# Rotary embedding and attention scores: the first batch loaded into a stage buffer, loads issued behind stores, q transposed early and k late in a step

## The chip, the cores and the metric

One core of a Trainium2 chip runs the whole program. The metric is the device time in microseconds (us) of one execution, the lower the better; a kernel's time is the median of several executions. Engines are named as the profile names them: PE (TensorE; PEld is its weight load), DVE (VectorE), ACT (ScalarE), POOL (GpSimd), SP (SyncE, which here does nothing but issue DMAs).

## What is computed

q and k have 16 batches, 512 positions, 16 heads and 64 numbers per head, all float32. Both get the rotary embedding, with one table of cosines and one of sines (512 positions by 32), and then every query position of a batch is multiplied with every key position, head by head:

```python
q1, q2 = q[..., :32], q[..., 32:]
q_rot = np.concatenate([q1 * cos - q2 * sin, q1 * sin + q2 * cos], axis=-1)
# k_rot: the same of k
scores = np.einsum('bshd,bthd->bsht', q_rot, k_rot)   # (16, 512, 16, 512), float32
```

The inputs are 67 MB in all and the output is 268 MB: four bytes leave the core for each that enters it.

## The kernel before

**Tiles and steps.** A *block* of q or k is 128 positions of one batch with all 16 heads, 128 partitions by 1024 numbers. There are 4 blocks in a batch (`C` = 4), and 64 in all (`NST`). Step `i` computes the scores of q block `i` against all 512 keys of its batch, in 8 pieces (`p` = 0 to 7, two heads each): `scores(i, p, st)` does two matmuls into one of three PSUM tiles `ps`, ACT copies that to the stage tile `st` (L166), and after the last piece SP issues one 4 MB store of `st` to the output (L171). There are three stage tiles, `stage_pool`, of 4 MB each; they are used in turn, and the first copy of a step waits until the store that last read its tile has landed.

**The first batch** is cut the other way. Its q and k are cut into four *units* of 4 heads each with all positions, so that the first scores need only one unit of each; a step's output is then stored in four parts of 1 MB (L169). The units are loaded by eight DMAs of 512 KB, `load_unit` (L79), into the same input tiles that later hold pairs of blocks.

**Loads.** From the second batch on, `load_pair` (L88) loads two neighbouring blocks with one DMA of 1 MB: into one of three tiles for k (`k_in`), one of two for q (`q_in`). A load waits until the embedding of the two blocks that were in the tile before is done.

**The embedding** of a block, `rope` (L115, L118, L121), is three DVE instructions: times cosine, times signed sine into `part`, and the sum. The signed sines, `ss_k` and `ss_q`, are made at the start by `build_table`, two small DVE instructions each (L59, L60).

**Transposes.** `transposed` turns 4 pieces of 128x128 of an embedded block on PE into a PSUM tile `bank` (there are two of them), which is then copied to `qT_t` or `kT_t`; a block takes two of these. In the first four steps `tr_act` does both halves of a unit, and ACT copies them (L176). From step 4 on DVE copies them (L259, in the first batch L215 for the key blocks of the second batch).

**The order of the work is written out by hand** (`tc.manual_schedule()`), and each engine runs its instructions in the order in which the program names them. SP issues DMAs in that order too, so a DMA that has to wait holds up those behind it. In steps 4 to 63 the order is: the load of this step (q at odd `i`, k at even `i`), then the eight pieces, with a transposed half after the pieces 0, 2, 3 and 5 (k, k, q, q), each followed by one embedding instruction on DVE and DVE's copy, and the rest of the embedding (q block `i`+2 and k block `i`+5) at the end. Within each step SP therefore has the load ahead of the store.

Of the kernel before, what the change touches and what calls it, by code (L numbers as in the profile page):

```python
# [10 lines left out]
def kernel(  # L11
# [8 lines left out]
    nc = tc.nc  # L20
# [5 lines left out]
    HD = D // 2  # L26
# [29 lines left out]
    def build_table(which):  # L56

        ss = const_pool.tile([P, C, 2, HD], fp32, name=f"ss_{which}")
        nc.vector.tensor_copy(out=ss[:, :, 0, :], in_=tabs["sin", which])  # L59
        nc.vector.tensor_scalar_mul(ss[:, :, 1, :], tabs["sin", which], -1.0)  # L60
        tabs["ss", which] = ss.rearrange("p c x j -> p c (x j)")

    in_tiles = {}
# [2 lines left out]
    def in_tile(which, pair):  # L66
        t = in_pool.tile(
            [P, 2, H * D], fp32, tag=which + "_in", bufs=IN_BUFS[which], name=which + "_sb"
        )
        in_tiles[which, pair] = t  # L70
        return t

    def load_unit(which, u):

        t = in_tiles.get((which, u // 2))
        if t is None:
            t = in_tile(which, u // 2)
        src = (k_v if which == "k" else q_v)[0, :, :, G * u : G * (u + 1), :]
        nc.sync.dma_start(t[:, u % 2].rearrange("p (c h d) -> p c h d", c=C, h=G), src)  # L79

    def load_pair(which, pair):

        b, x = divmod(pair, C // 2)
        if b >= B:
            return
        t = in_tile(which, pair)
        src = (k_v if which == "k" else q_v)[b, :, 2 * x : 2 * x + 2]
        nc.sync.dma_start(t.rearrange("p c (h d) -> p c h d", h=H), src)  # L88
# [3 lines left out]
    def rope(which, n):  # L92


        src = in_tiles[which, n // 2][:, n % 2]
        a = rot_pool.tile([P, H * D], fp32, tag="rot_" + which, name=which + "_rot")
        bt = rot_pool.tile([P, H * D], fp32, tag="part", name="part")
        cs, ss = tabs["cos", which], tabs["ss", which]
        if n < C:
            v1 = "p (c g j) -> p c g j"  # L100
            k1 = {"c": C, "j": HD}
            cs = cs.unsqueeze(2).to_broadcast((P, C, 2 * G, HD))
            ss = ss.unsqueeze(2).to_broadcast((P, C, G, D))
            k2 = {"c": C, "j": D}
        else:
            v1 = "p (g j) -> p g j"
            k1 = {"j": HD}
            cs = cs[:, n % C].unsqueeze(1).to_broadcast((P, 2 * H, HD))
            ss = ss[:, n % C].unsqueeze(1).to_broadcast((P, H, D))
            k2 = {"j": D}  # L110
        swapped = bass.AP(bt.tensor, bt.offset + HD, [bt.ap[0], (D, H), (-HD, 2), (1, HD)])
        a4 = a.rearrange("p (h x j) -> p h x j", x=2, j=HD)
        rots[which, n] = a
        return [
            lambda: nc.vector.tensor_tensor(  # L115
                a.rearrange(v1, **k1), src.rearrange(v1, **k1), cs, op=mult
            ),
            lambda: nc.vector.tensor_tensor(  # L118
                bt.rearrange(v1, **k2), src.rearrange(v1, **k2), ss, op=mult
            ),  # L120
            lambda: nc.vector.tensor_tensor(a4, a4, swapped, op=add),  # L121
        ]
# [50 lines left out]
    def tr_act(which, n):  # L173
        for g in range(2):
            bank, dst = transposed(which, n, g)
            nc.scalar.copy(out=dst, in_=bank)  # L176

    def run(ops):
        for op in ops:
            op()  # L180

    with tc.manual_schedule():
        load_tables("k", "(c p) j -> p c j")
        load_tables("q", "(p c) j -> p c j")
        for u in range(2):
            load_unit("k", u)
            load_unit("q", u)
        for which in ("k", "q"):
            for u in range(2, C):
                load_unit(which, u)  # L190
        load_pair("k", 2)
        make_identity(nc, ident)
        build_table("k")
        run(rope("k", 0))
        tr_act("k", 0)
        build_table("q")
        run(rope("q", 0))
        tr_act("q", 0)


        for i in range(C):
            st = stage_pool.tile([P, H, S], fp32, tag="stage", name="st")
            late = []
            if i > 0:
                late = [("k", C + i - 1, 0), ("k", C + i - 1, 1)]
            if i < C - 1:
                dve = rope("k", i + 1) + rope("q", i + 1) + rope("k", C + i)
            else:
                dve = rope("q", C) + rope("k", C + i) + rope("q", C + 1) + rope("k", 2 * C)
            for p in range(HP):  # L210
                scores(i, p, st)
                if p in (1, 2) and late:
                    bank, dst = transposed(*late.pop(0))
                    dve.pop(0)()
                    nc.vector.tensor_copy(out=dst, in_=bank)  # L215
                if p == 5:
                    run(dve[: 3 if i == 0 else 1])
                    dve = dve[3 if i == 0 else 1 :]
                    tr_act(*(("k", i + 1) if i < C - 1 else ("q", C)))
                if p == 7:  # L220
                    run(dve[:3])
                    dve = dve[3:]
                    tr_act(*(("q", i + 1) if i < C - 1 else ("k", C + i)))
            run(dve)
            if i == 0:
                load_pair("k", 3)
                load_pair("q", 2)
            elif i == 2:
                load_pair("k", 4)
                load_pair("q", 3)  # L230
                load_pair("k", 5)
            elif i == 3:
                load_pair("q", 4)
                load_pair("k", 6)


        for i in range(C, NST):
            tr = []
            if i + C < NST:
                tr += [("k", i + C, g) for g in range(2)]  # L240
            if i + 1 < NST:
                tr += [("q", i + 1, g) for g in range(2)]
            dve = []
            if i + 2 < NST:
                dve += rope("q", i + 2)
            if i + 1 + C < NST:
                dve += rope("k", i + 1 + C)
            if i % 2 == 1:
                load_pair("q", (i + 1) // 2 + 2)
            else:  # L250
                load_pair("k", (i + 4) // 2 + 3)
            st = stage_pool.tile([P, H, S], fp32, tag="stage", name="st")
            for p in range(HP):
                scores(i, p, st)
                if p in (0, 2, 3, 5) and tr:
                    bank, dst = transposed(*tr.pop(0))
                    run(dve[:1])
                    dve = dve[1:]
                    nc.vector.tensor_copy(out=dst, in_=bank)  # L259
            run(dve)  # L260


# [28 lines left out]
```

## Time and profile before

| what | before |
|---|---|
| median of 5 runs | 811.45 us (810.88 to 812.91) |
| the profiled execution, its own time | 811.71 us |
| span in its profile, first to last instruction | 809.9 us |
| PE busy | 677.5 us (84%) |
| DVE busy | 598.5 us (74%) |
| ACT busy | 500.7 us (62%) |
| bytes moved by DMA | 336.31 MB, 415 GB/s over the span |
| mean granted clock of PE | 0.951 |

How to read it: an engine's busy time is the union of its instructions' times. A table of windows gives, for stretches of the span, each engine's busy time and number of instructions, then the granted PE clock, the mean busy share of the 16 DMA engines, and the GB/s that they moved; in short windows the share can exceed 1, since a packet is counted where it starts. The chain of waits follows the execution back from its last instruction to what released each step.

### The profile page before, as it was taken

Reading aid. Unit: us, or ns where it says so; the run is one execution under the profiler, and the core shown is the slowest. Engines: PE = TensorE matmul, PEld = TensorE weight load, DVE = VectorE, ACT = ScalarE, POOL = GpSimd, SP = SyncE. Lnnn points to the kernel's source line nnn. Section 1 sums busy time; section 2 is a strip of 40 time slices with the busy share of each in tenths; the row PEclk is TensorE's granted clock in tenths of the full one; section 3 lists DMA queues with packets and bytes.
Section 4 is the critical chain, followed back from the end, with each engine's and each line's share of the span. In section 5 each row is a group of like instructions: output and inputs, shape, how many; then the busy total and the mean of one; then the engine's idle time right before and its main releaser. Section 6 shows DMA issues by size and latency. Waiting matters only on the chain.

```text
span 809.9 us, 7781 instructions
## 1 busy us (share of the span) xinstructions
PE 677.5 (84%) x3072; PEld 296.3 (37%) x3072; DVE 598.5 (74%) x624; ACT 500.7 (62%) x533; POOL 0.7 (0%) x6
## 2 busy tenths in 40 slices
PE   4997999888888888797988978888888879799870
PEld 2443444333333333343333433333333333344320
DVE  7798888887787787877868868678778787787300
ACT  3884777657556566575566656665656657566770
POOL 0000000000000000000000000000000000000000
PEclk9998999999999999999999999999999999999995
DMA  8999999999999999999999999999999999999994
GB/s 278 390 423 394 420 430 422 430 426 434 426 432 434 426 431 434 424 434 429 428 430 432 429 430 432 425 431 433 427 433 428 415 424 437 428 354 437 428 416 196
DMA packets 29028, 336.31 MB, mean 415 GB/s; under 512 B 3392, under 2 KB 7744, under 8 KB 15424
## 3 DMA queue, kind: packets, MB, share of 16 engines
q1 hardware_dynamic: 27648, 335.55, 98.2%
q8 instruction: 24, 0.39, 0.2%
q10 hardware_dynamic: 1344, 0.26, 0.2%
q14 instruction: 12, 0.10, 0.0%
HBM read 67.37 MB, written 268.44 MB: 415 GB/s over the span
## 4 chain that ended last, share of the span: by engine, by line
DMA 59%; PE 21%; DVE 8%; ACT 8%; issue 1%; ACTq 0%
DMA out_dram<-st 58%; PE ps L159 15%; ACT st L166 8%; PE bank L136 6%; DVE part L118 3%; DVE k_rot L121 2%; DVE k_rot L115 1%; DVE q_rot L121 1%; DVE q_rot L115 1%; DVE qT_t L259 1%; DMA sin_k<-in_sin_dram 0%; DVE kT_t L215 0%; ACT kT_t L176 0%; ACTq L286 0%; ACTq L166 0%
## 5 line engine op out<-in xcount | busy, mean ns | idle before, releaser
L166 ACT COPY st<-ps 128x1024 f32<-128x1024 f32 x512 | 489.5, 1021 | 275.6 <-DMA out_dram<-st 174.0
L159 PE MATMUL ps<-kT_t,qT_t 64*128 64x512 f32 x2048 | 528.8, 638 | 72.3 <-ACT st L166 69.8
L159 PEld LDWEIGHTS ps<-kT_t,qT_t 64*128 64x128 f32 x2048 | 182.3, 193 | 255.8 <-issue 148.5
L259 DVE COPY qT_t<-bank 128x512 f32<-128x512 f32 x118 | 81.5, 691 | 136.3 <-PE bank L136 135.8
L136 PE MATMUL bank<-ident,k_rot 128*128 128x128 f32 x512 | 84.5, 290 | 35.5 <-DVE k_rot L121 35.5
L136 PEld LDWEIGHTS bank<-ident,k_rot 128*128 128x128 f32 x512 | 55.0, 143 | 132.6 <-DVE k_rot L121 69.0
L136 PEld LDWEIGHTS bank<-ident,q_rot 128*128 128x128 f32 x512 | 58.9, 150 | 101.6 <-issue 78.9
L259 DVE COPY kT_t<-bank 128x512 f32<-128x512 f32 x112 | 77.0, 688 | 24.1 <-PE bank L136 24.1
L136 PE MATMUL bank<-ident,q_rot 128*128 128x128 f32 x512 | 90.6, 305 | 1.9 <-DVE q_rot L121 1.9
L121 DVE TENSOR_TENSOR k_rot<-k_rot,part 128x1024 f32<-128x1024 f32 x64 | 78.4, 1225 | 2.1
L121 DVE TENSOR_TENSOR q_rot<-q_rot,part 128x1024 f32<-128x1024 f32 x64 | 77.8, 1216 | 0.2
L115 DVE TENSOR_TENSOR q_rot<-q_sb,cos_q 128x1024 f32<-128x1024 f32 x64 | 77.9, 1218 | 0.0
L118 DVE TENSOR_TENSOR part<-k_sb,ss_k 128x1024 f32<-128x1024 f32 x64 | 77.8, 1216 | 0.0
L115 DVE TENSOR_TENSOR k_rot<-k_sb,cos_k 128x1024 f32<-128x1024 f32 x64 | 77.8, 1216 | 0.0
L118 DVE TENSOR_TENSOR part<-q_sb,ss_q 128x1024 f32<-128x1024 f32 x64 | 77.7, 1214 | 0.0
L176 ACT COPY kT_t<-bank 128x512 f32<-128x512 f32 x10 | 5.6, 619 | 6.5 <-PE bank L136 6.5
L176 ACT COPY qT_t<-bank 128x512 f32<-128x512 f32 x10 | 5.6, 617 | 2.6 <-PE bank L136 2.6
L215 DVE COPY kT_t<-bank 128x512 f32<-128x512 f32 x6 | 4.1, 684 | 4.1 <-PE bank L136 4.1
L59 DVE COPY ss_k<-sin_k 128x128 f32<-128x128 f32 x1 | 0.2, 227 | 5.2 <-DMA sin_k<-in_sin_dram 5.2
L176 ACT ACT_TABLE_LOAD x1 | 1.3, 1283 | 2.9 <-issue 2.9
masks.py:199 POOL TENSOR_SCALAR_AFFINE_SELECT ident<-ident 128x128 f32<-128x128 f32 x1 | 0.3, 293 | 0.1
L60 DVE TENSOR_SCALAR ss_k<-sin_k 128x128 f32<-128x128 f32 x1 | 0.2, 220 | 0.0
(7 smaller groups left out, 1.0 us busy)
## 6 DMA issues: line engine op xcount, KB each, us to landing
out_dram<-st SPq DMA_DIRECT2D x60, 4096.0 KB, 27.8
k_sb<-in_k_dram SPq DMA_DIRECT2D x30, 1024.0 KB, 19.9
q_sb<-in_q_dram SPq DMA_DIRECT2D x30, 1024.0 KB, 28.1
out_dram<-st SPq DMA_DIRECT2D x16, 1024.0 KB, 9.7
k_sb<-in_k_dram SPq DMA_DIRECT2D x4, 512.0 KB, 7.4
q_sb<-in_q_dram SPq DMA_DIRECT2D x4, 512.0 KB, 8.7
cos_k<-in_cos_dram ACTq DMA_DIRECT2D x1, 64.0 KB, 4.1
sin_k<-in_sin_dram ACTq DMA_DIRECT2D x1, 64.0 KB, 3.9
```

What stands on the lines that cost most here:

```text
L59: nc.vector.tensor_copy(out=ss[:, :, 0, :], in_=tabs["sin", which])
L60: nc.vector.tensor_scalar_mul(ss[:, :, 1, :], tabs["sin", which], -1.0)
L115: lambda: nc.vector.tensor_tensor(a.rearrange(v1, **k1), src.rearrange(v1, **k1), cs, op=mult),
L118: lambda: nc.vector.tensor_tensor(bt.rearrange(v1, **k2), src.rearrange(v1, **k2), ss, op=mult),
L121: lambda: nc.vector.tensor_tensor(a4, a4, swapped, op=add),
L136: nc.tensor.transpose(bank[:, x, :], src, ident)
L159: nc.tensor.matmul(out=ps[:, r, :], lhsT=lhs[64 * r : 64 * r + 64, :], rhs=rhs[64 * r : 64 * r + 64, :], start=True, stop=True,)
L166: nc.scalar.copy(out=st[:, 2 * p : 2 * p + 2, :], in_=ps)
L176: nc.scalar.copy(out=dst, in_=bank)
L215: nc.vector.tensor_copy(out=dst, in_=bank)
L259: nc.vector.tensor_copy(out=dst, in_=bank)
```

## The change

There are five parts to it.

1. `load_units` replaces `load_unit`: the first batch is loaded by four DMAs (4 heads of k, 4 of q, then the other 12 heads of k, 12 of q) into `early`, which takes the third stage tile. The input tiles are therefore free at the start, and the loads of k pair 2, q pair 2 and k pair 3 stand right behind the units on SP; k pair 4 and q pair 3 follow among the stores of step 0, k pair 5 behind step 1.
2. The two signed sine tables are built by ACT, both ahead of the first embedding.
3. In steps 0 to 3 the transposes of the next units come after the pieces 2 and 6 instead of 5 and 7, those of the second batch's keys after 0 and 1 instead of 1 and 2.
4. In steps 4 to 63 q is transposed after the pieces 1 and 3 and k after 5 and 6, and k's halves are copied by ACT instead of DVE.
5. In steps 4 to 63 the load is issued at the end of the step, behind its store on SP.

```diff
     def build_table(which):
         ss = const_pool.tile([P, C, 2, HD], fp32, name=f"ss_{which}")
-        nc.vector.tensor_copy(out=ss[:, :, 0, :], in_=tabs["sin", which])
-        nc.vector.tensor_scalar_mul(ss[:, :, 1, :], tabs["sin", which], -1.0)
+        nc.scalar.copy(out=ss[:, :, 0, :], in_=tabs["sin", which])
+        nc.scalar.mul(ss[:, :, 1, :], tabs["sin", which], -1.0)
...
+    st_first = [stage_pool.tile([P, H, S], fp32, tag="stage", name="st") for _ in range(2)]
+    early = stage_pool.tile([P, 2 * C * H * D], fp32, tag="stage", name="early")
+    units = {}
+
+    def load_units(which, head, heads):
+        n = C * heads * D
+        t = early[:, load_units.used : load_units.used + n]
+        load_units.used += n
+        t = t.rearrange("p (c e) -> p c e", c=C)
+        src = (k_v if which == "k" else q_v)[0, :, :, head : head + heads, :]
+        nc.sync.dma_start(t.rearrange("p c (h d) -> p c h d", d=D), src)
+        for h in range(0, heads, G):
+            units[which, (head + h) // G] = t[:, :, D * h : D * (h + G)]
...
-        for u in range(2):
-            load_unit("k", u)
-            load_unit("q", u)
-        for which in ("k", "q"):
-            for u in range(2, C):
-                load_unit(which, u)
+        for head, heads in ((0, G), (G, H - G)):
+            load_units("k", head, heads)
+            load_units("q", head, heads)
         load_pair("k", 2)
+        load_pair("q", 2)
+        load_pair("k", 3)
         make_identity(nc, ident)
         build_table("k")
+        build_table("q")
         run(rope("k", 0))
         tr_act("k", 0)
-        build_table("q")
...
         for i in range(C):
...
-                if p in (1, 2) and late:
+                if p in (0, 1) and late:
                     bank, dst = transposed(*late.pop(0))
                     dve.pop(0)()
                     nc.vector.tensor_copy(out=dst, in_=bank)
-                if p == 5:
-                    run(dve[: 3 if i == 0 else 1])
-                    dve = dve[3 if i == 0 else 1 :]
-                    tr_act(*(("k", i + 1) if i < C - 1 else ("q", C)))
-                if p == 7:
-                    run(dve[:3])
-                    dve = dve[3:]
-                    tr_act(*(("q", i + 1) if i < C - 1 else ("k", C + i)))
+                if i == 0 and p == 1:
+                    load_pair("k", 4)
+                if i == 0 and p == 3:
+                    load_pair("q", 3)
+                if p in (2, 6):
+                    m = len(dve) - (6 if p == 2 else 3) + (-3 if i == C - 1 else 0)
+                    run(dve[:m])
+                    dve = dve[m:]
+                    tr_act(*nxt.pop(0))
             run(dve)
-            if i == 0:
-                load_pair("k", 3)
-                load_pair("q", 2)
-            elif i == 2:
-                load_pair("k", 4)
-                load_pair("q", 3)
+            if i == 1:
                 load_pair("k", 5)
...
         for i in range(C, NST):
-            tr = []
+            tr = {}
+            if i + 1 < NST:
+                tr[1], tr[3] = ("q", i + 1, 0), ("q", i + 1, 1)
             if i + C < NST:
-                tr += [("k", i + C, g) for g in range(2)]
-            if i + 1 < NST:
-                tr += [("q", i + 1, g) for g in range(2)]
+                tr[5], tr[6] = ("k", i + C, 0), ("k", i + C, 1)
...
-            if i % 2 == 1:
-                load_pair("q", (i + 1) // 2 + 2)
-            else:
-                load_pair("k", (i + 4) // 2 + 3)
             st = stage_pool.tile([P, H, S], fp32, tag="stage", name="st")
             for p in range(HP):
                 scores(i, p, st)
-                if p in (0, 2, 3, 5) and tr:
-                    bank, dst = transposed(*tr.pop(0))
+                if p not in tr:
+                    continue
+                bank, dst = transposed(*tr[p])
+                if tr[p][0] == "q":
                     run(dve[:1])
                     dve = dve[1:]
                     nc.vector.tensor_copy(out=dst, in_=bank)
+                else:
+                    nc.scalar.copy(out=dst, in_=bank)
             run(dve)
+            if i % 2 == 1:
+                load_pair("q", (i + 1) // 2 + 2)
+            else:
+                load_pair("k", (i + 4) // 2 + 3)
```

## The prediction, written before the changed kernel had run

> **What bounds the kernel now.** I read the page's rates first, then a table of windows, then the chain of waits, then SP's waits. The busy shares decide nothing here: PE's 84% is spread over 810 us, and the queue of DMAs is full almost throughout.
>
> From a table of windows (PE, PEld, DVE, ACT, POOL busy, then PE clock, DMA share, GB/s):
>
> ```profile
> 6.00:14.00 8.00, 2.90 (x13) 2.56 (x14) 7.93 (x10) 1.17 (x2) 0.00 (x0) 1.00 1.10 353
> 18.00:19.00 1.00, 1.00 (x8) 0.43 (x6) 0.97 (x2) 0.98 (x3) 0.00 (x0) 1.00 0.09 37
> 19.00:20.00 1.00, 1.00 (x6) 0.38 (x4) 1.00 (x2) 1.00 (x3) 0.00 (x0) 1.00 0.14 57
> 28.00:30.00 2.00, 2.00 (x13) 1.06 (x12) 1.29 (x2) 1.42 (x3) 0.00 (x0) 1.00 1.03 324
> 30.00:32.00 2.00, 2.00 (x11) 0.96 (x11) 2.00 (x3) 1.37 (x2) 0.00 (x0) 1.00 0.91 287
> 34.00:36.00 2.00, 2.00 (x11) 0.72 (x9) 1.97 (x3) 2.00 (x4) 0.00 (x0) 1.00 1.00 315
> ...
> 78.00:79.00 1.00, 0.99 (x6) 0.16 (x2) 0.97 (x2) 1.00 (x2) 0.00 (x0) 1.00 0.64 258
> 79.00:80.00 1.00, 0.61 (x6) 0.44 (x6) 1.00 (x2) 1.00 (x2) 0.00 (x0) 1.00 0.85 119
> ...
> 150.00:700.00 550.00, 470.95 (x2122) 204.66 (x2120) 422.42 (x443) 337.27 (x355) 0.00 (x0) 0.96 1.01 429
> ...
> 800.00:804.00 4.00, 0.00 (x0) 0.00 (x0) 0.00 (x0) 0.00 (x0) 0.00 (x0) 0.50 0.06 25
> 804.00:808.00 4.00, 0.00 (x0) 0.00 (x0) 0.00 (x0) 0.00 (x0) 0.00 (x0) 0.50 0.06 25
> ```
>
> For 550 us the transfers run at 429 GB/s with a share of 1: nothing but the DMA engines limits that stretch, and nothing that PE, DVE or ACT do faster can shorten it. What is left is at the ends. The first loads run at 353 GB/s; the queue is nearly empty from 18.8 to 20.0 and thin from 78.3 to about 80; and from 28 to 36 it is slow three times for a reason that I don't see. The last two rows matter as much: a share of 0.06 is one engine of sixteen. One DMA engine finishes 9 us after the others. It is served in the order of issue like the rest and always has work after 80 us, so the end is set by the bytes that this one engine has to move, plus the time in which even it had none.
>
> From the chain of waits, 152 to 230 us, and from SP's waits:
>
> ```profile
> 152.69 28.89 DMA out_dram<-st
> ...
> 181.68 1.02 ACT st L166
> ...
> 190.02 28.76 DMA out_dram<-st
> ```
>
> ```profile
> SPq L286 <- DMA out_dram<-st: 20.2, 1, 20.2
> ```
>
> A store is issued 8.3 us after the store three steps before has landed (181.68 to 190.02), and then takes 28.8 us, of which its own 4 MB need only 9.9 (4.19 MB at 425 GB/s). The rest is queue: two other stores and a load or two stand ahead. So a step's compute may finish some 17 us later than it does before the queue runs dry. The last store still lands 20 us after its issue, so the last steps' compute is hidden too.
>
> Two rows of the timeline carry the gap at 79 us:
>
> ```profile
> 66.33 1.09 PE L136 MATMUL bank<-ident,k_rot 128*128 128x128 f32 x4 [4.30 <-DVE k_rot L121]
> 79.28 0.36 SPq L171 DMA_DIRECT2D out_dram<-st  x1
> ```
>
> Step 4 issues its store only at 79.28, when the queue has been emptied. It lost time because its first transpose is of k block 8, whose embedding is the last thing DVE does in step 3: PE stands 4.30 us, and its granted clock then falls (0.81 from 60 to 78 us).
>
> **The change part by part**, against the profiled execution (span 809.9, itself 811.71, which is 0.26 above the median of 811.45; differences carry over).
>
> *Larger packets in the first loads.* Before, all 4.19 MB come as rows of 1 KB (4 heads), at 353 GB/s. After, a quarter does, and 3.15 MB come as rows of 3 KB. No row shows 3 KB; from below it is the 1 KB row's 353, from above the stores' 429, and the nearest is k's 4 KB rows (window 60 to 78, mostly 8 KB and 4 KB: 421), so I take 410. 3.15 MB take 7.7 us instead of 8.9: **1.2 us less**, between 0 and 1.6. All queued behind moves up by that.
>
> *The loads brought forward.* q pair 2 and k pair 3 (2.1 MB, 5 us) now stand directly behind the units. The queue lasts until about 20.0 - 1.2 - 1.2 + 5.0 = 22.6, and the first store is issued at about 19 as before (19.11). The hole of 18.8 to 20.0 is filled: **1.2 us less**. The bytes are the same, only moved; k pair 4 and q pair 3 fall among step 0's stores and wait for no tile, so no store is held behind them.
>
> *Signed sines on ACT.* DVE loses four instructions of 0.22 us, about 0.8 us ahead of the second embedding; ACT gains four that end before its first copy at 10.37. The trace speaks of sin_q, the last table: 6.3 us from issue to landing. [...]
>
> *Steps 0 to 3.* DVE sets their pace: nine embedding instructions and two copies are 9 x 1.17 + 2 x 0.65 = 11.8 us, and a step took 11.6. That stays. The third stage tile holds the first batch until its last embedding (about 44), so step 2 must wait for step 0's stores: they now end at about 22.6 + 6 MB at 425 = 37.5, when step 2's first copy is due at 38 to 39 (38.87 before). That is close, so 0 to 1 us of ACT waiting, hidden as long as the queue holds.
>
> *Step 4.* q block 5 comes first, ready some 3.6 us earlier than k block 8, and k after piece 5. Pieces 0 to 5 no longer stand still. From ACT's first copy at about 62.4, eight copies at 0.96 to 1.02 and two of k at 0.6 make 9.3 us: the store goes out at about 72, not 79.28. The queue, with the savings above, is dry at about 77. **The gap, 1.3 us on the slowest engine** (1.6 by the mean rate of 78 to 82), is gone.
>
> *k's copies on ACT.* DVE loses 112 x 688 ns = 77 us of busy time; ACT gains 112 at about 0.6 (L176: 0.62) = 67 us. Per step DVE falls to 6 x 1.22 + 2 x 0.69 = 8.7, ACT rises to 8 x 1.0 + 1.2 = 9.2, PE stays near 10 of busy time. All are below the 12.4 of a step ((227.22 - 152.69) / 6), so **0**; the stores' issue comes about 1 us later after the tile is free.
>
> *Loads behind stores.* Each load is behind one more store in the queue, 9.9 us. The bytes don't change: **0** unless a load is late. k has five steps before its use. q is used three steps later: the load of step i lands some 2.5 us after store i, and store i's landing is also what lets step i+3 begin. So every other step DVE's first embedding waits about 2.5 us, and behind it in its order the copy of q's half, then PE's k transpose (which needs that bank), then ACT's copy of k. DVE then ends at 2.5 + 8.7 = 11.2 of 12.4 us, the store at about 10.5 instead of 8.3. The two stores still queued cover this; without them it would cost 2 us each second step, some 55 us.
>
> *The slow stretches of 28 to 36.* Short of 430 GB/s by 2 x (106 + 143 + 115) / 430 = 1.7 us. Nothing says that they stay or go; bounds 0 and 1.7, or as much again lost. I count 0.7 as gained.
>
> Sum: 1.2 + 1.2 + 1.3 + 0.7 = 4.4 us, so **807.1** for the median (span 805.5).
>
> **The rivals.**
>
> *The gaps close only in part (19%).* Step 4 comes at 78 or later, and 2.4 to 3.1 us are won: 808.4 to 809.0. For it: steps 0 to 3 are paced by one engine, and PE now waits for it at piece 2. Against it: 5 us between 72 and 77.
>
> *The gain never reaches the slowest engine (10%).* If its 9 us come from something other than its bytes and its empty time, the closed gaps serve the other fifteen, which wait at the end anyway. Only part of the first 1.2 us counts: 810.2 to 811.5. Against it: it too lacked work at 19 and 79.
>
> *The start becomes too slow for the queue (10%, slower).* In steps 0 to 3 PE reaches piece 2 about 1.2 us before the embedding that it must transpose there is done; everything behind it on PE stands still. If that adds to DVE's pace instead of overlapping it, four steps cost about 5 us, and ACT's wait for step 0's stores 1 more: step 4's store comes near 79. Should the slow 0.81 clock return there (half speed on eight pieces, about 4 us), it comes at 83, and the queue is empty for 83 + 1 - 77 = 7 us where I assume none: 811.45 + 7 - 3.1 = 815. It decides from about 81 on. Against it: the trace shows DVE without idle from 29 to 66.
>
> *The reordering of steps 4 to 63 does nothing for the time*: that is part of my main case, not of its cost.
>
> **How the numbers follow.** This kernel's five runs stretch over 0.25%, so 0.2%, 1.6 us, is about what a measurement can tell from no change. The main case (all three gaps closed, 61%) gives 805.2 (mean-rate sizes and all of the slow stretches: 1.2 + 1.8 + 1.6 + 1.7 = 6.3) to 808.3. With the partial case it is faster: 0.80. Same 0.10, slower 0.10. The range leaves out the far side of the slower case: 805.2 to 810.8.
>
> **What would show it.** Right: 400 GB/s or more from 16 to 27 us; step 4's store before 76 and no dip behind it; DVE busy near 520 us, ACT near 567; q_rot waiting for q_sb in about every other step; 429 GB/s from 150 to 700; and still one engine alone in the last 9 us. Wrong: an empty queue between 20 and 90 us, or any window of the long stretch below 425.

## The result and the profile after

| what | before | after |
|---|---|---|
| median of the runs | 812.00 us (43 runs) | 809.21 us (25 runs, 805.03 to 812.86) |
| ratio after/before | | 0.9965, 95% interval 0.9955 to 0.9975 |
| the profiled execution, its own time | 811.71 us | 807.30 us |
| span in its profile | 809.9 us | 805.5 us |
| DVE / ACT busy | 598.5 / 500.7 us | 523.2 / 561.3 us |

The changed kernel is 2.8 us faster by the medians; the forecast was 4.4, with a range of 805.2 to 810.8 us, in which the 809.21 lies. The profiled execution, with 4.4 us less of span, is one of the three quickest of the 25. The executions of the changed kernel lie further apart than those of the one before, so single profiles are read here for where things happen, and medians for how much they are worth.

The table of windows of the changed kernel, at the places that were shown of before (us; busy time of PE, PEld, DVE, ACT, POOL with instruction counts, granted clock, DMA share, GB/s):

```profile
6.00:14.00 8.00, 2.13 (x9) 1.79 (x10) 6.32 (x7) 2.19 (x6) 0.00 (x0) 1.00 1.03 391
18.00:19.00 1.00, 1.00 (x4) 0.33 (x2) 1.00 (x2) 0.82 (x1) 0.00 (x0) 1.00 0.98 410
19.00:20.00 1.00, 1.00 (x6) 0.19 (x2) 0.97 (x2) 0.65 (x1) 0.00 (x0) 1.00 0.96 393
24.00:28.00 4.00, 4.00 (x23) 1.81 (x20) 1.38 (x2) 4.00 (x7) 0.00 (x0) 1.00 0.99 369
28.00:30.00 2.00, 2.00 (x14) 0.91 (x11) 1.62 (x2) 1.42 (x2) 0.00 (x0) 1.00 1.02 434
84.00:90.00 6.00, 6.00 (x32) 2.63 (x28) 4.29 (x6) 4.91 (x6) 0.00 (x0) 1.00 0.83 283
150.00:700.00 550.00, 478.36 (x2116) 201.07 (x2116) 361.01 (x352) 385.16 (x442) 0.00 (x0) 0.95 1.01 430
796.00:800.00 4.00, 0.00 (x0) 0.00 (x0) 0.00 (x0) 0.00 (x0) 0.00 (x0) 0.50 0.08 33
800.00:804.00 4.00, 0.00 (x0) 0.00 (x0) 0.00 (x0) 0.00 (x0) 0.00 (x0) 0.50 0.06 25
```

The first loads run at 391 GB/s instead of 353. The hole of 18.8 to 20.0 is filled. A slow stretch is still there, at 24 to 28 (369 GB/s), and a larger one at 84 to 90 (283), where the first 4 MB store and the k load behind it are on their way. The long stretch is at 430, as before. At the end one sixteenth of the DMA capacity is busy: from 798.7 us on, when the second latest has landed its last bytes, the one late engine is alone for 6 us (share 0.06 from 800 to 804).

The store of step 4 in the timeline, then rows of the waits (us in total, times, longest), then groups of the page (busy time, mean ns of one, idle time before and what ended it):

```profile
73.90 0.34 SPq L184 DMA_DIRECT2D out_dram<-st  x1
```

```profile
DVE q_rot L128 <- DMA q_sb<-in_q_dram: 163.6, 27, 8.1
ACT st L179 <- DMA out_dram<-st: 142.4, 52, 5.0
```

```profile
L128 DVE TENSOR_TENSOR q_rot<-q_sb,cos_q 128x1024 f32<-128x1024 f32 x60 | 73.3, 1222 | 163.6 <-DMA q_sb<-in_q_dram 163.6
L269 ACT COPY kT_t<-bank 128x512 f32<-128x512 f32 x112 | 66.9, 597 | 0.0
```

Step 4's store goes out 5.4 us earlier than before, and k's copies on ACT cost the 0.6 us each that was assumed. New is the wait of DVE for q: 163.6 / 27 = 6.1 us every other step. The forecast had 2.5.

**Landing times.** Below, "latest landing" is the last of the sixteen updates of a DMA's semaphore in the trace; "median" is the eighth. Each update is read as one DMA engine's: while the last store of all lacks only its last update, the DMA share is one sixteenth (0.06 from 800 to 804 us, before and after). They show what the mean GB/s hide: how far the one late engine is. Its lag behind the second latest at the end of the program was 8.99 us before and 5.94 after. The trace does not name the engines; that the latest landings belong to one and the same engine is read from their even distances.

### The profile page after: what moved, and what is told of

The parts are those of the page before. It is cut to its first block, busy times and chain, and to the rows that moved or that the text cites. A ratio compares the mean times of both kernels' runs of the same rounds, so it can differ in the third digit from the quotient of the medians.

```text
span 805.5 us, 7719 instructions
## 1 busy us (share of the span) xinstructions
PE 684.7 (85%) x3072; PEld 293.0 (36%) x3072; DVE 523.2 (65%) x508; ACT 561.3 (70%) x649; POOL 0.7 (0%) x6
## 4 chain that ended last, share of the span: by engine, by line
DMA 62%; PE 26%; ACT 6%; DVE 2%; issue 1%; ACTq 0%; SPq 0%
DMA out_dram<-st 58%; PE ps L172 19%; PE bank L149 7%; ACT st L179 5%; DMA q_sb<-in_q_dram 4%; DMA sin_k<-in_sin_dram 1%; DVE part L131 1%; DVE kT_t L229 0%; DVE q_rot L128 0%; DVE q_rot L134 0%; DVE k_rot L134 0%; ACTq L300 0%; ACTq L179 0%; DVE qT_t L267 0%; ACTq L53 0%
## 5 line engine op out<-in xcount | busy, mean ns | idle before, releaser
L172 PE MATMUL ps<-kT_t,qT_t 64*128 64x512 f32 x2048 | 542.6, 643 | 81.4 <-ACT st L179 81.4
L128 DVE TENSOR_TENSOR q_rot<-q_sb,cos_q 128x1024 f32<-128x1024 f32 x60 | 73.3, 1222 | 163.6 <-DMA q_sb<-in_q_dram 163.6
L128 DVE TENSOR_TENSOR k_rot<-k_sb,cos_k 128x1024 f32<-128x1024 f32 x60 | 73.1, 1218 | 0.0
L131 DVE TENSOR_TENSOR part<-k_sb,ss_k 128x1024 f32<-128x1024 f32 x60 | 73.0, 1217 | 0.0
L131 DVE TENSOR_TENSOR part<-q_sb,ss_q 128x1024 f32<-128x1024 f32 x60 | 72.9, 1215 | 0.0
L269 ACT COPY kT_t<-bank 128x512 f32<-128x512 f32 x112 | 66.9, 597 | 0.0
L128 DVE TENSOR_TENSOR k_rot<-early,cos_k 128x1024 f32<-128x1024 f32 x4 | 4.9, 1220 | 4.8 <-DMA cos_k<-in_cos_dram 4.8
L189 ACT COPY kT_t<-bank 128x512 f32<-128x512 f32 x10 | 5.5, 602 | 2.5 <-PE bank L149 2.5
L229 DVE COPY kT_t<-bank 128x512 f32<-128x512 f32 x6 | 4.1, 688 | 3.4 <-PE bank L149 3.4
L131 DVE TENSOR_TENSOR part<-early,ss_k 128x1024 f32<-128x1024 f32 x4 | 4.9, 1218 | 1.6 <-ACT ss_k L60 1.6
L131 DVE TENSOR_TENSOR part<-early,ss_q 128x1024 f32<-128x1024 f32 x4 | 4.9, 1218 | 0.0
L128 DVE TENSOR_TENSOR q_rot<-early,cos_q 128x1024 f32<-128x1024 f32 x4 | 4.9, 1218 | 0.0
```

Of the source, the lines that this page charges most:

```text
L128: lambda: nc.vector.tensor_tensor(a.rearrange(v1, **k1), src.rearrange(sv, j=HD), cs, op=mult),
L131: lambda: nc.vector.tensor_tensor(bt.rearrange(v1, **k2), src.rearrange(sv, j=D), ss, op=mult),
L172: nc.tensor.matmul(out=ps[:, r, :], lhsT=lhs[64 * r : 64 * r + 64, :], rhs=rhs[64 * r : 64 * r + 64, :], start=True, stop=True,)
```

## The experiments

All ratios are to the kernel before as it ran beside each kernel on the same chip, with 95% intervals; 0.001 is 0.8 us. They are not quotients of the medians, from which they differ by up to 0.0014. Each of three groups is of one chip of its own: the three parts alone and the middle store; parts 1 and 4, all but part 4, all but part 5 and the last store; and the rows of 1 KB, the loads not brought forward and the values marked "again".

| kernel | ratio |
|---|---|
| early loads alone (part 1) | 0.9988 (0.9977 to 0.9999) |
| order of steps 4 to 63, k by ACT alone (part 4) | 0.9989 (0.9976 to 1.0001) |
| loads behind stores alone (part 5) | 0.9989 (0.9975 to 1.0003) |
| parts 1 and 4 | 0.9948 (0.9932 to 0.9964) |
| all but part 4 | 0.9961 (0.9951 to 0.9970) |
| all but part 5 | 0.9950 (0.9930 to 0.9969), again 0.9944 (0.9931 to 0.9957) |
| all | 0.9965 (0.9955 to 0.9975), again 0.9962 (0.9949 to 0.9976) |
| all, first loads with rows of 1 KB | 0.9994 (0.9982 to 1.0006) |
| all, loads not brought forward | 0.9974 (0.9961 to 0.9986) |
| all, a middle store cut 120 + 8 | 1.0259 (1.0227 to 1.0291) |
| all, the last store cut 120 + 8 | 1.0071 (1.0045 to 1.0097) |

### One part alone: early loads

```diff
...
+        for head, heads in ((0, G), (G, H - G)):
+            load_units("k", head, heads)
+            load_units("q", head, heads)
         load_pair("k", 2)
+        load_pair("q", 2)
+        load_pair("k", 3)
...
-            if i == 0:
-                load_pair("k", 3)
-                load_pair("q", 2)
```

> The kernel before with the first part of the change alone: the first batch goes into the third stage tile in rows of 1 KB and 3 KB, and q pair 2 and k pairs 3 and 4, q pair 3 are loaded early; the order of the transposes, k's copies on DVE, the signed sines on DVE and the place of the loads from step 4 on stay as before. Theory (what counts is the bytes of the slowest DMA engine and the time in which it has none): the first units land 1.2 us sooner and the hole of 18.8 to 20.0 us closes, so 2.4 us less (-0.3%), the mean rate from 18 to 20 us is above 380 GB/s, and step 4's store still goes out near 79 us or later, so nothing more is won there. Rival (the closed hole serves only engines that wait at the end anyway): within 1 us of before. Rival (the third stage tile is missed in step 2): slower, with ACT waiting for the first stores near 38 us and step 4's store after 81.

Measured: 811.44 us against 811.95, 0.1% faster, where the theory had 2.4 us: the rival's number. Its reason does not fit, for the latest engine did get the gain. The early gain was there: k pair 6, the last transfer ahead of step 4, landed at 77.47 on the latest engine instead of 80.66, 3.2 us earlier. Then the windows of this kernel show what became of it:

```profile
76.00:77.00 1.00, 1.00 (x6) 0.21 (x4) 1.00 (x2) 0.54 (x1) 0.00 (x0) 1.00 0.10 41
77.00:78.00 1.00, 1.00 (x8) 0.63 (x8) 0.39 (x2) 1.00 (x2) 0.00 (x0) 1.00 0.00 0
78.00:79.00 1.00, 1.00 (x6) 0.47 (x6) 1.00 (x2) 0.42 (x2) 0.00 (x0) 1.00 0.00 0
79.00:80.00 1.00, 1.00 (x6) 0.39 (x4) 0.97 (x2) 1.00 (x2) 0.00 (x0) 1.00 0.00 0
80.00:81.00 1.00, 0.63 (x4) 0.00 (x0) 1.00 (x2) 1.00 (x2) 0.00 (x0) 1.00 0.40 61
```

```profile
79.74 0.38 SPq L96 DMA_DIRECT2D k_sb<-in_k_dram  x1
80.92 0.36 SPq L182 DMA_DIRECT2D out_dram<-st  x1
```

Not a byte moves for three microseconds. PE is busy all through them, and DVE and ACT for most of them, so the queue is waiting for step 4 to be computed; its store came even 1.6 us later than before (80.92 for 79.28). By the time step 4's store and k pair 7 had both landed, this kernel was 1.2 us behind the one before (95.46 against 94.22). Bytes brought forward are worth little if the next store isn't.

### One part alone: order and k by ACT

```diff
-            tr = []
+            tr = {}
+            if i + 1 < NST:
+                tr[1], tr[3] = ("q", i + 1, 0), ("q", i + 1, 1)
             if i + C < NST:
-                tr += [("k", i + C, g) for g in range(2)]
-            if i + 1 < NST:
-                tr += [("q", i + 1, g) for g in range(2)]
+                tr[5], tr[6] = ("k", i + C, 0), ("k", i + C, 1)
...
+                else:
+                    nc.scalar.copy(out=dst, in_=bank)
```

> The kernel before with the fourth part of the change alone: from step 4 on q is transposed after the pieces 1 and 3, k after 5 and 6, and k's halves are copied by ACT; loads stay ahead of the stores. Theory: step 4's store goes out near 72 instead of 79 us, the gap behind it closes, 1.3 us less (-0.16%), DVE busy near 520, ACT near 565, and the long stretch stays at 429 GB/s. Rival (the slow stretch near 80 us in the traces of both kernels is not an empty queue: the load of k pair 7 was slow in the changed kernel too, 4.8 us for 2.5): no change of the time although the store comes 7 us sooner.

Measured: 811.99 us against 811.95; the interval includes no change, but it does not exclude the 1.3 us of the theory either (0.9984). Step 4's store went out at 74.56 instead of 79.28, but the latest engine still had k pair 6 to finish until 81.85, as in the kernel before (80.66), and the two next transfers landed at 94.66 (94.22 before). Before, k pair 7 had been issued at 78.11, ahead of 80.66, and so the latest engine had no gap near 79 that an earlier store could close. The fifteen others had. What the latest engine did lose there is the 1.3 us by which k pair 7 took longer than the 2.5 of k pair 6 (80.66 to 84.50 for 78.16 to 80.66), and the trace shows slow packets there: up to 0.76 us for 4 KB between 80 and 83, where the median of all packets of that size is 0.16. With the new order k pair 7 took 3.1 us (81.85 to 84.91).

### One part alone: loads behind stores

```diff
-            if i % 2 == 1:
-                load_pair("q", (i + 1) // 2 + 2)
-            else:
-                load_pair("k", (i + 4) // 2 + 3)
             st = stage_pool.tile([P, H, S], fp32, tag="stage", name="st")
...
             run(dve)
+            if i % 2 == 1:
+                load_pair("q", (i + 1) // 2 + 2)
+            else:
+                load_pair("k", (i + 4) // 2 + 3)
```

> The kernel before with the fifth part of the change alone: from step 4 on each load is issued behind its step's store. Theory: the slowest DMA engine moves the same bytes and always has work, so the time is that of before within 1 us, though DVE now waits for q in every other step (27 waits, some 6 us each as in the changed kernel, 160 us in all). Rival (the loads' place is what wins or loses time): over 2 us either way, seen as a rate that differs from 429 GB/s between 150 and 700 us.

Measured: 811.17 us against 811.95; the interval includes no change, and a cost of 1.6 us is outside it. So on the kernel before, this part alone does no harm that can be seen. The waits for q were there, 4.5 us each instead of the 6 expected:

```profile
DVE q_rot L115 <- DMA q_sb<-in_q_dram: 116.4, 26, 5.9
```

### Two parts together

The kernel is the kernel before with the edits of the first two experiments, both.

> The kernel before with two parts of the change and no other: the early loads (units in two sizes, k pairs 2 and 3 and q pair 2 at once) and the new order of steps 4 and later with k's copies on ScalarE. Steps 0 to 3, the tables on VectorE and the loads ahead of the store are left as before. Alone the first gave a ratio of 0.9988 and the second 0.9989. Theory A (the two only pay together, because the early loads move every later byte forward only if step 4's store is out before the queue is empty): ratio 0.9965 or a little under, a profiled span of 805 to 807, step 4's store issued by 76. Rival B (the parts add up without any need of each other): 0.9988 x 0.9989 = 0.9977, a span near 808. Rival C (the order of steps 0 to 3 and the tables on ScalarE carry a part of it): over 0.998.

Measured: 807.60 us, ratio 0.9948, where the sum of the two alone would be 0.9977. Theory A is borne out, and by more than it said: the parts need each other. (Part 4 is two edits, the order and k's copies on ACT; which of them counts was not tried.) Step 4's store is issued at 73.81, ahead of the time at which k pair 6 lands, 77.11:

```profile
73.34 0.38 SPq L96 DMA_DIRECT2D k_sb<-in_k_dram  x1
73.81 0.42 SPq L182 DMA_DIRECT2D out_dram<-st  x1
```

```profile
74.00:78.00 4.00, 4.00 (x20) 1.71 (x20) 4.00 (x6) 2.90 (x4) 0.00 (x0) 1.00 1.00 239
78.00:80.00 2.00, 2.00 (x11) 0.74 (x9) 2.00 (x3) 2.00 (x3) 0.00 (x0) 1.00 1.09 410
```

The DMA engines are busy throughout (share 1.00), though at 239 GB/s for 4 us: there is no gap, but the slow stretch around the first 4 MB store is here too. And parts 2, 3 and 5, absent here, are not needed for the gain.

### All but the order

```diff
-            tr = {}
+            tr = []
+            if i + C < NST:
+                tr += [("k", i + C, g) for g in range(2)]
             if i + 1 < NST:
-                tr[1], tr[3] = ("q", i + 1, 0), ("q", i + 1, 1)
-            if i + C < NST:
-                tr[5], tr[6] = ("k", i + C, 0), ("k", i + C, 1)
+                tr += [("q", i + 1, g) for g in range(2)]
...
+                if p in (0, 2, 3, 5) and tr:
...
-                else:
-                    nc.scalar.copy(out=dst, in_=bank)
```

> The changed kernel with one part undone: steps 4 and later have their transposes where the kernel before has them, and k's banks are moved out by VectorE again. Theory A: step 4's store goes out at 80 or later, the queue empties near 77.5 as it did with the early loads alone (k pair 7 was the last transfer then, landing 8.2 us after its forerunner), and the early gain is given back: ratio 0.9985 to 0.9995, span 809 to 810. Rival B (parts add up): without the 0.1% of the order the ratio is 0.9975. Rival C (the order is worth nothing to the start): 0.9965.

Measured: 808.50 us, ratio 0.9961: not Theory A's 0.9985 or more, but Rival C's value. The store did not come at 80 or later: it is issued at 78.05, and with the loads behind the stores the load of k pair 7 follows it, at 78.49. The windows:

```profile
74.00:76.00 2.00, 2.00 (x12) 1.03 (x12) 1.41 (x3) 1.52 (x2) 0.00 (x0) 1.00 0.27 111
76.00:78.00 2.00, 1.77 (x10) 0.47 (x6) 1.97 (x2) 1.90 (x3) 0.00 (x0) 1.00 0.07 31
78.00:79.00 1.00, 0.83 (x6) 0.67 (x8) 1.00 (x2) 0.94 (x2) 0.00 (x0) 1.00 1.02 422
```

From 76 to 78 the mean share is 0.07, about one engine of sixteen (0.0625). Fifteen engines stand still; the late one is still working off k pair 6, until 79.64, and the store reaches it in time. In this profile it goes from there to the landing of the store, 90.28, in 10.6 us, hardly more than the 9.7 that the same store took in the profile of the changed kernel (77.72 to 87.41). A hole on fifteen engines that the late one doesn't see cost nothing here. So Theory A has to be put more narrowly: what decides is whether the next transfer reaches the *latest* engine before that one is empty. With the early loads alone the next transfer of any kind came 2.3 us too late (79.74 against 77.47), and the store after that; here the store came 1.6 us ahead. It could be otherwise in an execution in which that engine's lag at 78 is smaller than the 2.8 us of this profile.

### All but the loads behind stores

```diff
+            if i % 2 == 1:
+                load_pair("q", (i + 1) // 2 + 2)
+            else:
+                load_pair("k", (i + 4) // 2 + 3)
             st = stage_pool.tile([P, H, S], fp32, tag="stage", name="st")
...
             run(dve)
-            if i % 2 == 1:
-                load_pair("q", (i + 1) // 2 + 2)
-            else:
-                load_pair("k", (i + 4) // 2 + 3)
```

> The changed kernel with one part undone: in steps 4 and later each load of a pair is issued ahead of its step's matmuls again, not behind its store. The 163.6 us for which VectorE waits for q pairs (27 times, 6.1 us each) should vanish to under 20 us. Theory A (these waits are covered by the stores that stand in the queue): ratio 0.9965, within 0.001 of the changed kernel, although more than 140 us of waits have gone. Rival D (the waits cost the end something): 0.995 or less. Rival E (the loads behind stores keep the slowest DMA engine busier): 0.998 or more.

Measured: 807.38 us, ratio 0.9950. The waits for q pairs are gone from the list of waits; the ratio is at Rival D's bound, and its interval overlaps that of the changed kernel. So it was run again, with the changed kernel beside it.

> The changed kernel itself, to stand beside the others of this group on one chip: ratio 0.9965 as measured at first, 0.9955 to 0.9975.

> The changed kernel with the loads ahead of the matmuls again (as the run in which VectorE's waits for q pairs vanished), beside the changed kernel itself. Theory A (those waits are covered): equal within 0.001. Rival D (loads behind stores cost the end something): it is 0.0010 to 0.0020 under the changed kernel, as the first measurement suggested (0.9950 against 0.9965, on different chips, with intervals that overlap).

Measured: the changed kernel 809.21 us (0.9962), and with loads ahead 807.48 us (0.9944). The means differ by 1.58 us, with a standard error of 0.65 worked out from the two sets of times (9 and 6). With two measurements saying the same, Rival D's number holds: loads behind stores cost about 1.6 us in the changed kernel. That they cost it through the waits for q is not shown: with this part alone there were 116 us of such waits, and no cost. In the profile with loads ahead another wait has taken the place of that for q pairs (163.6 us):

```profile
DVE qT_t L271 <- PE bank L149: 230.1, 115, 5.1
```

DVE idles nearly as long as in the changed kernel (278.5 us of the span, against 282.3 and 287.7 in the two profiles of that), and the time is still shorter: the sum of DVE's waits is no measure of their cost.

Where the 1.6 us go, the windows narrow down and do not settle. The changed kernel in this second profile (span 810.3; the slowest of its nine executions, so it shows more than 1.6 us), and then the one with loads ahead (span 805.3):

```profile
190.00:490.00 300.00, 262.14 (x1162) 109.94 (x1158) 196.89 (x192) 210.21 (x243) 0.00 (x0) 0.95 1.01 430
490.00:640.00 150.00, 129.35 (x570) 54.43 (x572) 97.41 (x96) 103.72 (x120) 0.00 (x0) 0.94 1.00 421
640.00:740.00 100.00, 86.32 (x390) 36.23 (x386) 66.36 (x65) 70.18 (x82) 0.00 (x0) 0.96 0.98 399
```

```profile
190.00:490.00 300.00, 261.32 (x1156) 109.80 (x1156) 198.61 (x192) 210.34 (x242) 0.00 (x0) 0.95 1.01 430
490.00:640.00 150.00, 129.61 (x580) 54.56 (x576) 99.30 (x96) 104.73 (x121) 0.00 (x0) 0.95 1.01 429
640.00:740.00 100.00, 90.43 (x414) 38.53 (x412) 69.16 (x67) 74.89 (x87) 0.00 (x0) 0.97 0.98 411
```

From 190 to 490 they are equal. After that the changed kernel falls to 421 and 399 where the other has 429 and 411; in the shortfall the share of busy DMA stays at 1.00 and 0.98, so the packets take longer. But the changed kernel's first profile, of a quick execution, has 430 and 407 in the same two windows, and the first one with loads ahead 425 and 406. The late slow stretches differ from one execution to the next in either kernel. That they come more often with the loads behind, because the waits leave fewer stores queued, would fit and is not shown.

### Rows of 1 KB in the first loads

```diff
-        for head, heads in ((0, G), (G, H - G)):
-            load_units("k", head, heads)
-            load_units("q", head, heads)
+        for head in range(0, H, G):
+            load_units("k", head, G)
+            load_units("q", head, G)
```

> The changed kernel, with its first loads cut into eight of 512 KB (rows of 1 KB, as before) and not into two of 512 KB and two of 1536 KB (rows of 3 KB). Everything else, the loads brought forward too, stays. It measures the term 'larger packets, 1.2 us' by itself. If the term is right, the last of these loads lands at 16.8 on the latest DMA engine (it was 16.77 before and 15.54 after the change), and k pair 6 lands 1.2 us later than in the changed kernel, near 78.9; the ratio to the kernel before is 0.0015 above that of the changed kernel in this same group. Rival: the loads' order and not their rows made them early; then they land at 15.5 and the ratio is that of the changed kernel. The rows of 1 KB at 353 GB/s speak for the first.

Measured: the last unit lands at 16.60 on the latest engine (15.54 in the changed kernel's first profile, 15.22 in its second), and the window of 6 to 14 us is back at 348 GB/s, where the 3 KB rows had 391:

```profile
6.00:14.00 8.00, 2.48 (x11) 2.14 (x12) 6.68 (x7) 2.19 (x6) 0.00 (x0) 1.00 1.06 348
```

So it is the rows (or the number of DMAs, which goes with them), and not the order. The time is 810.30 us against 809.21 for the changed kernel in this group: 1.1 by the medians, 2.1 by the means (standard error 0.7), and 0.0032 by the ratios, where 0.0015 was expected. They differ because eight of its 22 executions lie apart from the rest, at 813.3 to 814.5; why is not known. One part of the expectation missed: k pair 6 landed at 77.29, not at 78.9, within what two profiles of the changed kernel differ by (77.72 and 75.90).

### Loads not brought forward

```diff
         load_pair("k", 2)
-        load_pair("q", 2)
-        load_pair("k", 3)
...
-                if i == 0 and p == 1:
-                    load_pair("k", 4)
-                if i == 0 and p == 3:
-                    load_pair("q", 3)
...
-            if i == 1:
+            if i == 0:
+                load_pair("k", 3)
+                load_pair("q", 2)
+            elif i == 2:
+                load_pair("k", 4)
+                load_pair("q", 3)
                 load_pair("k", 5)
```

> The changed kernel, with k pair 3 and q pair 2 issued after step 0 and k pair 4, q pair 3 and k pair 5 after step 2, as the kernel before has them; the first loads keep their rows of 3 KB. It measures the term 'loads brought forward, 1.2 us' by itself. If the term is right, the rate falls below 250 GB/s in a window of 1 to 3 us between 17 and 21 us (the queue is empty at 18, the first store comes at 20.4), k pair 6 lands 1.5 to 3 us later than the changed kernel's 77.7, and the ratio is 0.002 to 0.0035 above that of the changed kernel in this group, near 0.998. Rival: the hole is filled by nothing that the latest engine needed, and the ratio stays within 0.001 of the changed kernel's.

Measured: 809.83 us, ratio 0.9974: 0.0012 above the changed kernel, 0.6 us by the medians and 1.0 by the means (standard error 0.7). That is less than the 0.002 expected and just over the rival's 0.001, so it decides for neither. The hole is as foretold, and longer than before the change, since the loads ahead of it end earlier:

```profile
17.00:18.00 1.00, 1.00 (x4) 0.34 (x2) 1.00 (x2) 0.73 (x1) 0.00 (x0) 1.00 0.06 25
18.00:19.00 1.00, 1.00 (x6) 0.19 (x2) 0.97 (x2) 0.70 (x1) 0.00 (x0) 1.00 0.00 0
19.00:20.00 1.00, 1.00 (x10) 0.86 (x8) 1.00 (x2) 1.00 (x2) 0.00 (x0) 1.00 0.00 0
```

k pair 6 landed at 82.26, 4.5 us after the changed kernel's 77.72, more than the 3 expected. That this came to only 1 us or less in the time is not explained here; the profiled execution, 811.85, is the slowest of this kernel's seven.

### A store cut into 120 and 8 partitions

```diff
-            nc.sync.dma_start(o_v[b, i % C], st)
+            if i in (32,):
+                nc.sync.dma_start(o_v[b, i % C][:120], st[:120])
+                nc.sync.dma_start(o_v[b, i % C][120:], st[120:])
+            else:
+                nc.sync.dma_start(o_v[b, i % C], st)
```

That is the middle one; for the last store the condition is `i == NST - 1`.

> The changed kernel with one store, that of step 32, issued as two DMAs: 120 partitions and then the last 8. [...] Rival (the end is set by the mean rate of all sixteen): no change wherever the slow engine is.

> The changed kernel, with the last store of all (4 MB) cut into one of partitions 0 to 119 and one of partitions 120 to 127, so that one of the sixteen DMA engines gets nothing of the first part. The same cut in the middle of the kernel made it 22 us slower and much of the queue ran at half its speed for 60 us, so there it could not say which engine is late. Here nothing is queued behind it. The lag of the latest engine was 5.9 us at the end of the changed kernel's profile, and its share of the last store is 9.7 us. Theory F (one engine alone is late, and it is the one that is left out): the time falls by the lag less what the other engines lose, by 2 to 5 us, ratio 0.991 to 0.994. Rival G (the late engine is another one): it has 0 or 1.2 us more to do, ratio 0.9965 to 0.998. Rival H (the cut slows the packets of all, as in the middle, where many took 2.5 us and not 1.2): 0.998 to 1.01.

Measured: 834.01 us for the middle store, where the rival had no change, and 818.18 for the last, which Theory F had quicker. In the trace of the last one the 120 partitions give fifteen landings and the 8 give eight, so one engine has no part in the first, but with the cut the packets are slower. The middle one, before and behind the cut, and then the last one:

```profile
380.00:400.00 20.00, 17.74 (x86) 7.67 (x84) 15.70 (x16) 14.24 (x17) 0.00 (x0) 1.00 1.01 428
420.00:440.00 20.00, 9.57 (x38) 3.94 (x36) 4.75 (x6) 7.04 (x9) 0.00 (x0) 0.76 0.98 298
```

```profile
770.00:780.00 10.00, 6.46 (x28) 1.89 (x24) 0.00 (x0) 7.74 (x9) 0.00 (x0) 1.00 1.02 436
780.00:800.00 20.00, 0.00 (x0) 0.00 (x0) 0.00 (x0) 0.01 (x1) 0.00 (x0) 0.58 0.84 241
```

A busy share of 0.98 at 298 GB/s means that packets take longer, not that they are missing: from 415 to 440 us a fifth of the 32 KB packets took 2.4 us or more, up to 5.0, where the median of that size is 1.21 in the traces of before and after. (It was not half the speed for 60 us, as the second expectation has it: from 420 to 480 us the rate was 228 to 397 GB/s in stretches of 10 us. The lowest, at 460 to 470, is a queue that had run half empty, share 0.55.) In the last store's case even the whole store ahead of the cut one, which was still in the queue, took 17.5 us on the latest engine (782.32 to 799.81) instead of 10, and that engine then had its full 9.7 us of the 120 partitions still to do: it was not the one left out. It is one of the eight that carry the last 8 partitions too: their last landing is 810.70, 1.2 us after its 809.50, while the other seven were done at 802.29. Rival H for the size, Rival G for the engine. Which of the eight is late, and why, stays open.

## Why the prediction was right, and where not

The sign was right and the size somewhat too large: 2.8 us instead of 4.4. By its number alone the result is nearest to the rival of gaps that close only in part (808.4 to 809.0), but that one had step 4's store at 78 or later, and it came at 73.90. Step by step:

- **What bounds the kernel: right.** One late engine sets the end. From the 9th to the 33rd of the 4 MB stores (some 190 to 490 us) its landings are 298.6 us apart before, 298.8 after and 298.8 with the loads ahead, 12.4 us a step, although 75 us of busy time went off DVE and 61 onto ACT. In these kernels everything won or lost lies ahead of 190 us and behind 490. (The other profiles have 296.5 to 299.0; the shortest are the early loads alone and the loads behind alone, in which a second engine was late beside the first.) The rival that the gain never reaches that engine is out.
- **Larger packets, 1.2 us: right.** The units land 1.2 us earlier in the profile (16.77 to 15.54), and undoing this alone costs 1.1 by the medians, 2.1 by the means.
- **Loads brought forward, 1.2 us: right in kind, perhaps too large.** The hole is filled; undoing this alone costs 0.6 to 1.0, and the standard error of 0.7 doesn't exclude 1.2.
- **Signed sines on ACT: no term in the sum, and no cost that was seen.** sin_q, 6.3 us from issue to landing before, landed at 8.53 to 8.73 in the four profiles with 1 KB rows and at 8.86 to 9.91 in all those with 3 KB rows, 0.7 us later in the mean; why is not shown. The first store came at 17.73 to 20.39 and not at "about 19". In the changed kernel's profile, where it came at 20.39, that was covered: k pair 3 landed at 23.10, and from 18 to 20 us the DMA share was 0.98 and 0.96.
- **Steps 0 to 3, 0: right, as far as it was tried.** Parts 2 and 3 were not undone by themselves, but parts 1 and 4 without them (0.9948) are as fast as with them and without part 5 (0.9950 and 0.9944).
- **Step 4, 1.3 us: the store was right (73.90 where 72 was worked out), the price was not.** The prediction counts 1.3 us of empty time near 79 on the slowest engine, which had none: k pair 7 was issued at 78.11 and its forerunner landed on that engine at 80.66; what it lost behind that went into slow packets. Alone, the order is worth nothing that can be measured (though 1.3 us is not excluded there). What it does is to keep the gap from opening once the early loads have pulled the queue forward: with the loads ahead of the stores that is the difference between 0.9988 and 0.9948, 3.2 us. With the loads behind the stores the load no longer stands ahead of step 4's store, and there the order added nothing (0.9961 without it, 0.9962 and 0.9965 with it). The terms were added as if each stood by itself, but the early ones keep their worth only if step 4's transfers come in time.
- **Slow stretches, 0.7 us: not earned.** They moved. From 84 to 90 the changed kernel is short by 6 x (430 - 283) / 430 = 2.1 us, and a stretch of that kind lies near the first 4 MB store in other kernels too (239 GB/s at 74 to 78 above). The one from 84 to 90 is where 1 us of the early 2.9 (k pair 6 at 77.72 instead of 80.66) was lost by 94 us (92.22 against 94.22), and one of the prediction's signs of being right, no dip behind step 4's store, failed there.
- **k's copies on ACT, 0: right.** DVE 523.2 for the forecast 520, ACT 561.3 for 567.
- **Loads behind stores, 0: this step failed.** The mechanism was named, DVE waiting for q every other step, but at 2.5 us where it is 6.1, and with "the two stores still queued cover this". The runs with the loads ahead, 0.9950 and 0.9944, put the cost at about 1.6 us, nearly all of what the forecast was too high by; by which way they cost it stays open. Those two kernels came in at 807.4 and 807.5, the predicted 807.1 almost. That is luck in part: the sum has 1.3 us for step 4 and 0.7 for the slow stretches, and the runs show neither by itself, but 3.2 us for the early loads and the order together beyond the early loads alone.

The changed kernel with its loads left ahead, 807.4 to 807.5 us, is faster than both kernels; the early loads and the order alone, 807.6 us, do as well.

## What to carry to other kernels

When a transfer engine sets the end, read the gaps on that engine, by its own landings, and not in the mean rate: here a hole on fifteen of sixteen engines cost nothing (share 0.07 from 76 to 78 us, ratio 0.9961), and closing one by the order alone won nothing that can be measured (0.9989, 0.9976 to 1.0001). Bringing transfers forward paid here only as far as the next transfer was ready too; so test such parts in pairs as well as alone, since here two parts of 0.1% each gave 0.5% together. And a wait that is said to be covered by a queue should be tried without it: the part that brought this one looked free by itself, and still cost 0.2% in company.

## What the runs showed of the hardware

- **A store of 120 + 8 partitions is no small change of the same bytes.** One such store among sixty cost 22 us in the middle of the kernel and 6 us at its end, both against the kernel before (25 and 9 against the changed one), with many 32 KB packets of 2.4 us and more instead of 1.21. Whether it is the fifteen engines or the two DMAs for one that does it was not tried.
- **One DMA engine of sixteen fell behind in the long stretch.** In ten of the twelve profiles with uncut stores its lag behind the second latest grew from under 2 us near 100 us to 8 to 12 us near 700, and was 6 to 9 us at the end. In the other two a second engine fell behind with it: with the early loads alone the two ended 7 and 11 us behind the median. In the profile with the last store cut it is one of the eight engines that the 8 partitions used: their last landing was at 810.70, the other seven by 802.29.
- **The rate falls for some 4 to 8 us near the first 4 MB store**, to 239 GB/s in one kernel (74 to 78 us, parts 1 and 4) and 283 in another (84 to 90, the changed one), with packets that take longer (in the latter 0.22 us in the mean for 4 KB, where it was 0.16 from 150 to 700). It is clear in eight of the twelve profiles with uncut stores, somewhere from 72 to 96 us, and weak in four; the changed kernel's own two profiles are one of each, so it differs between executions. Its cause was not tried.
